# A product-key gate table built from three bf16 products per token instead of one fp32 product, and 64 instead of 48 expert chunks parked beside it

## The chip, the cores and the metric

One core of one Trainium2 chip. The time is the device time of one execution in microseconds (us), as the median of three runs. The engines are TensorE (PE in the rows; PEld is its weight load), VectorE (DVE), ScalarE (ACT), GpSimd (POOL) and SyncE (SP), which issues most DMAs.

## The reference

One transformer layer over 512 tokens of width 1024: attention and a gated recurrence in parallel, merged, then a product-key mixture of 16384 single-neuron experts (8 heads, 16 experts each per token), then a gated embedding. The part that matters here is the mixture:

```python
s = jnp.einsum('thpc,hpnc->thpn', q, sub_keys)      # 2 x 128 key scores per head
v1, i1 = lax.top_k(s[:, :, 0], 16)
v2, i2 = lax.top_k(s[:, :, 1], 16)
...                                                 # 16 best of the 256 sums: idx = 128 * i1 + i2
g = jax.nn.softmax(top_s, axis=-1)
ue = jnp.take(u, idx, axis=0)                       # 128 rows of u per token
a = jnp.einsum('thkd,td->thk', ue, x)
w = jax.nn.gelu(a) * g
ve = jnp.take(v, idx, axis=0)
out = jnp.einsum('thk,thkd->td', w, ve)
```

## The kernel before

The first 128 tokens take the mixture by gathering: for each of 128 slots an indirect DMA fetches one row of u per token (tile gu), VectorE multiplies and sums it (L849), and later the same with v (gv, L858). The other 384 tokens take it densely: all 16384 experts, in 128 chunks of 128, are computed for every token and multiplied by a gate table that is zero except at the chosen experts.

A dense chunk is `dense_a`: its weights (u_raw, 512 KB, 128x1024) are split by ScalarE into u_h and by VectorE into the rest u_l (`split`, L139 and L140), 24 fp32r matmuls of 384 columns (`mm3`, L134 to L136, three for each of 8 slices) fill the PSUM tile pa, and ScalarE's gelu (L742) writes ge, 128x384. The second half of a chunk, in the loop over `it` from 0 to 127, loads the rows of v, splits them, multiplies ge by the chunk's part of the gate table (gch, loaded for 8 chunks at a time from DRAM), splits the product into w_h and w_l, and adds 18 matmuls of 512 columns into six PSUM banks po.

The gate table must be whole before the second halves can start. While it is built, TensorE gets first halves of chunks to do: SP of them (48) are parked, that is, ge is written to DRAM (adram) and read back later (ges). The remaining 80 chunks have their first half inside the loop over `it`, up to 8 ahead (PRE). `chunk_order` spreads the parked chunks among the others.

The table is built in this order: `topk` (VectorE, tb 0 and 1: selection of the experts), then for each of the three blocks of 128 dense tokens `build`, with the selection of the next block woven in (`zipped`). In `build` a block is transposed (L811), and its first index, second index and gates land in tij and gr with the token on the free axis. For 8 tokens at a time (TQ), VectorE compares an iota with the first index (gL, fp32 one-hots, L823) and with the second (gO, bf16, L825), ScalarE multiplies each token's gO by its gate (gR, fp32, L827), and TensorE multiplies the two over the 128 slots: one fp32 matmul of 128 columns per token into pg (L832), which runs as two instructions in the trace. ScalarE copies pg, four tokens at a time, into gs (L834). After 32 tokens gs goes to DRAM (gdram, L836). pg, gL, gO and gR have two buffers each.

The loop over `units()` sets the order: each step of selection or building yields a cost, and a chunk is issued whenever the summed cost passes another APACE (3.3). Gathers of u are issued by the same sum. The generators' costs are not touched by the change. Within an engine, instructions run in their written order.

Of the kernel before, what the change touches and what calls it, by code (L numbers as in the profile page):

```python
# [8 lines left out]
F32 = mybir.dt.float32  # L9
F32R = mybir.dt.float32r  # L10
BF16 = mybir.dt.bfloat16
I32 = mybir.dt.int32
U32 = mybir.dt.uint32
AF = mybir.ActivationFunctionType
OP = mybir.AluOpType
# [16 lines left out]
GB = 32  # L32
# [14 lines left out]
TD = T - NG  # L47
NTB = TD // GB
PRE = 8
SP = 48  # L50
TQ = 8
APACE = 3.3
GPACE = 0.4
GSTART = 30
GS2 = 135
# [22 lines left out]
def chunk_order():  # L78
    spilled, fresh = [], []
    for c in range(128):  # L80
        ns, nf = SP - len(spilled), 128 - SP - len(fresh)
        (spilled if ns and (c < S0 or not nf or ns * (128 - SP) >= nf * SP) else fresh).append(c)
    return {c: i for i, c in enumerate(spilled)}, spilled + fresh
# [29 lines left out]
def zipped(*gens):  # L113
    gens = [[0.0, i, g] for i, g in enumerate(gens)]
    while gens:
        e = min(gens)
        try:
            c = next(e[2])
        except StopIteration:
            gens.remove(e)  # L120
            continue
        e[0] += c
        yield c


def body(nc, tc, I, out, taps=None, stop=99):
# [17 lines left out]
    with contextlib.ExitStack() as top:  # L144
# [563 lines left out]
        if stop <= 5:  # L708
            ul_st.close()
            return  # L710
        peer(nc, tc, I, out, xd, cst, gains, norm_T1, rstd_of, split, mm3, tap, stop, pp, ha, la, h2n, v8s, i8s, st, top,
             idxg, gg, acc, aa, ul_st, up, u_split, u_pre)


def peer(nc, tc, I, out, xd, cst, gains, norm_T1, rstd_of, split, mm3, tap, stop, pp, ha, la, h2n, v8s, i8s, st, top,
         idxg, gg, acc, aa, ul_st, up, u_split, u_pre):
    import contextlib
    V, S, PE, G, DM = nc.vector, nc.scalar, nc.tensor, nc.gpsimd, nc.sync
    ident = cst[:, C_ID:C_ID + 128]
    iota = cst[:, C_IOTA:C_IOTA + 128]  # L720
# [3 lines left out]
    if True:  # L724
        dp = st.enter_context(tc.tile_pool(name="gdram", bufs=1, space=bass.MemoryType.DRAM))
        gd = dp.tile([NTB, 128, 128 * GB], F32, name="gdram")
        ad = dp.tile([SP, 128, TD], F32, name="adram")
        ys = contextlib.ExitStack()
# [5 lines left out]
        def dense_a(c):  # L734
            uh, ul = u_pre.pop(c, None) or u_split(c)
            pa = psa.tile([128, TD], F32, name="pa", tag="pa")
            for k in range(ND):
                e = slice(k * 128, (k + 1) * 128)
                mm3(pa, uh[:, e], ul[:, e], ha[:, k, NG:T], la[:, k, NG:T], k == 0, k == ND - 1)
            ge = gp.tile([128, TD], F32, name="ge", tag="ge")  # L740
            with tc.high_priority(HPG):
                S.activation(ge, pa, AF.Gelu_apprx_tanh)  # L742
            return ge
# [64 lines left out]
        def build(kp, bp, ps, tb, i_f, g_o, iob):  # L808
            pt = ps.tile([128, 3, 128], F32, name="pt3", tag="pt3", bufs=1)
            for i, s in enumerate((i_f[:, 0, :], i_f[:, 1, :], g_o)):  # L810
                PE.transpose(pt[:, i, :], s, ident)  # L811
            tij = kp.tile([128, 2, 128], BF16, name="tij", tag="tij")
            S.activation(tij, pt[:, 0:2, :], AF.Copy)
            gr = kp.tile([128, 128], F32, name="gr", tag="gr")
            S.activation(gr, pt[:, 2, :], AF.Copy)
            for b in range(128 // GB):
                gs = bp.tile([128, 128, GB], F32, name="gs", tag="gs", bufs=1)
                for q8 in range(GB // TQ):
                    t0 = b * GB + q8 * TQ
                    LL = bp.tile([128, TQ, 128], F32, name="gL", tag="gL")  # L820
                    OO = bp.tile([128, 128, TQ], BF16, name="gO", tag="gO")
                    RR = bp.tile([128, TQ, 128], F32, name="gR", tag="gR")
                    V.tensor_tensor(LL, iob[:, :, 0][:, None, :].to_broadcast([128, TQ, 128]),  # L823
                                    tij[:, 0, t0:t0 + TQ, None].to_broadcast([128, TQ, 128]), op=OP.is_equal)
                    V.tensor_tensor(OO, iob, tij[:, 1, None, t0:t0 + TQ].to_broadcast([128, 128, TQ]), op=OP.is_equal)  # L825
                    for t in range(TQ):
                        S.activation(RR[:, t, :], OO[:, :, t], AF.Copy, scale=gr[:, t0 + t:t0 + t + 1])  # L827
                    for q4 in range(TQ // 4):
                        pg = ps.tile([128, 4, 128], F32, name="pg", tag="pg")
                        for w in range(4):  # L830
                            t = q4 * 4 + w
                            PE.matmul(pg[:, w, :], RR[:, t, :], LL[:, t, :], start=True, stop=True)  # L832
                        o = q8 * TQ + 4 * q4
                        S.activation(gs[:, :, o:o + 4].rearrange("p i t -> p t i"), pg, AF.Copy)  # L834
                    yield TQ * 0.21 + 0.1
                DM.dma_start(gd[(tb - TB0) * (128 // GB) + b], gs.rearrange("p i t -> p (i t)"))  # L836
# [25 lines left out]
        def gathers(nu, nv, dve=None, act=None):  # L862
            with tc.issue_after(dve.ins) if dve else contextlib.nullcontext():
                while cnt["u"] < min(128, nu):
                    slot_u(cnt["u"])
                    cnt["u"] += 1
            if nv is None:
                return
            while cnt["w"] < 128 and (cnt["u"] >= cnt["w"] + WG + WLAG or (cnt["u"] == 128 and nu >= 128 + WLAG)):
                with tc.issue_after(act.ins) if act else contextlib.nullcontext():  # L870
                    slot_w(cnt["w"])
                cnt["w"] += WG
            with tc.issue_after(dve.ins) if dve else contextlib.nullcontext():
                while cnt["v"] < min(cnt["w"], nv):
                    slot_v(cnt["v"])
                    cnt["v"] += 1

        with s7:
            kp = s7.enter_context(tc.tile_pool(name="topk", side="right", **LR))
            bp = s7.enter_context(tc.tile_pool(name="gbld", side="right", bufs=2, reuse_waits="tile"))  # L880
            ps = s7.enter_context(tc.psum_pool(name="psg", side="right", bufs=2, reuse_waits="tile"))
            iob = kp.tile([128, 128, TQ], BF16, name="iob")
            V.tensor_copy(iob, iota[:, :, None].to_broadcast([128, 128, TQ]))
            i16 = kp.tile([128, 16, NK], BF16, name="i16")
            V.tensor_copy(i16, iota[:, 0:16, None].to_broadcast([128, 16, NK]))

            def sel(tb):
                i_f = kp.tile([128, 2, NK], F32, name="i_f", tag="i_f", bufs=2)
                g_o = kp.tile([128, NK], F32, name="g_o", tag="g_o", bufs=2) if tb >= TB0 else gg
                sels[tb] = i_f, g_o  # L890
                yield from topk(kp, tb, i_f, g_o, i16)
                if tb < TB0:
                    idx_f = kp.tile([128, NK], F32, name="idx_f", tag="idx_f")
                    V.scalar_tensor_tensor(idx_f, i_f[:, 0, :], 128.0, i_f[:, 1, :], op0=OP.mult, op1=OP.add)
                    V.tensor_copy(idxg, idx_f)
                    tap("idx", idx_f)
                    tap("g", gg)

            sels = {}

            def units():
                yield from sel(0)
                yield from sel(1)
                for tb in (1, 2, 3):
                    gens = [build(kp, bp, ps, tb, *sels[tb], iob)]
                    if tb < 3:
                        gens.append(sel(tb + 1))
                    yield from zipped(*gens)

            na, cost = 0, 0.0  # L910
            pend = []

            def next_a(c):
                ge = dense_a(c)
                if c < SP:
                    DM.dma_start(ad[c], ge)
                else:
                    pend.append(ge)

            for _ in range(A0):  # L920
                next_a(na)
                na += 1
            for u in units():
                cost += u
                while cost > (na + 1 - A0) * APACE and na < SP + NPE:
                    next_a(na)
                    na += 1
                if cost > GSTART:
                    gathers((cost - GSTART) * GPACE + max(0.0, cost - GS2) * GP2, None)
            GW = cnt["u"]  # L930
            print("COST", cost, na, GW) if DBG else None
            while na < SP + NPE:
                next_a(na)
                na += 1
# [123 lines left out]
        with contextlib.ExitStack() as e2:  # L1058
            pe2.append(e2.enter_context(tc.tile_pool(name="ple3", side="right", **LR)))
            ps = e2.enter_context(tc.psum_pool(name="psp", side="right", bufs=4, reuse_waits="tile"))  # L1060
            for n in range(4):
                w = wg0 if n == 0 else load_wg(n)
# [60 lines left out]
```

## Time and profile before

| | us |
|---|---|
| median of three runs | 1925.13 |
| lowest and highest | 1924.31, 1926.99 |
| span of the profiled execution | 1926.0 |

The page gives the profiled execution by its span, from the first to the last instruction. By the stretches, the first 605 us are the projections, attention, recurrence and the queries; the selections and the table take until about 1010 us; the loop over `it` runs until about 1840 us; the embedding gate ends it. A busy time counts an instruction as long as it is recorded; matmuls overlap one another, so the distance between their starts says more than their length. Of a group, the mean length follows the busy time, and then the idle time of the engine just before, with what ended it.

### The profile page before, as it was taken

Reading aid. Unit: us, or ns where it says so; the run is one execution under the profiler, and the core shown is the slowest. Engines: PE = TensorE matmul, PEld = TensorE weight load, DVE = VectorE, ACT = ScalarE, POOL = GpSimd, SP = SyncE. Lnnn points to the kernel's source line nnn. Section 1 sums busy time; section 2 is a strip of 40 time slices with the busy share of each in tenths; the row PEclk is TensorE's granted clock in tenths of the full one; section 3 lists DMA queues with packets and bytes.
Section 4 is the critical chain, followed back from the end, with each engine's and each line's share of the span. In section 5 each row is a group of like instructions: output and inputs, shape, how many; then the busy total and the mean of one; then the engine's idle time right before and its main releaser. Section 6 shows DMA issues by size and latency. Waiting matters only on the chain.

```text
span 1926.0 us, 27936 instructions
## 1 busy us (share of the span) xinstructions
PE 1849.9 (96%) x10349; PEld 1641.7 (85%) x10349; DVE 1415.6 (73%) x2893; ACT 985.6 (51%) x1563; POOL 376.2 (20%) x260
## 2 busy tenths in 40 slices
PE   6999999999999999888889999999999999999998
PEld 6997878888998988777778889888888888888888
DVE  4689777444888999988746778877788777756464
ACT  5755657532533588998994333333333333333443
POOL 0000000000000222214200334444354443200000
PEclk9999999999999999999999999999999999999999
DMA  4212100433321776777749998988899888865512
GB/s 160 78 56 76 44 12 23 129 105 130 128 78 53 256 249 245 275 256 259 258 155 311 358 321 315 336 326 312 326 334 344 309 310 319 277 216 182 190 58 85
DMA packets 133944, 397.49 MB, mean 206 GB/s; under 512 B 12848, under 2 KB 52016, under 8 KB 132144
## 3 DMA queue, kind: packets, MB, share of 16 engines
q1 hardware_dynamic: 96944, 261.48, 39.4%
q0 software_dynamic: 36864, 134.23, 19.7%
q8 instruction: 81, 1.33, 0.3%
q14 instruction: 55, 0.45, 0.1%
HBM read 356.86 MB, written 38.80 MB: 205 GB/s over the span
## 4 chain that ended last, share of the span: by engine, by line
PE 46%; ACT 8%; DMA 2%; DVE 1%; issue 1%; ACTq 0%; SPq 0%
PE po L136 9%; PE po L135 9%; PE po L134 9%; PE pa L136 5%; PE pa L134 5%; PE pa L135 5%; ACT gR L827 4%; ACT gs L834 3%; DMA gdram<-gs 1%; ACT u_h L139 1%; PE pg L134 1%; PE pg L136 1%; PE pg L135 1%; DMA gchg<-gdram 1%; PE pg L832 0%
## 5 line engine op out<-in xcount | busy, mean ns | idle before, releaser
L843 POOL DMA_INDIRECT gu<-in_peer_u_dram,idxg x128 | 188.8, 1475 | 1137.5 <-DVE cd L766 662.9
L136 PE MATMUL pa<-ha,u_l 128*128 128x384 f32 x1024 | 349.6, 341 | 6.6 <-DVE u_l L140 6.6
L134 PE MATMUL pa<-ha,u_h 128*128 128x384 f32 x1024 | 349.4, 341 | 1.8 <-ACT u_h L139 1.8
L135 PE MATMUL pa<-la,u_h 128*128 128x384 f32 x1024 | 349.1, 341 | 0.0
L134 PE MATMUL po<-v_h,w_h 128*128 128x512 f32 x768 | 299.3, 390 | 1.8 <-ACT w_h L139 1.8
L135 PE MATMUL po<-v_l,w_h 128*128 128x512 f32 x768 | 300.8, 392 | 0.0
L136 PE MATMUL po<-v_h,w_l 128*128 128x512 f32 x768 | 300.7, 392 | 0.0
L139 ACT ACTIVATE u_h<-u_raw 128x1024 fp32r<-128x1024 f32 x128 | 136.1, 1064 | 203.4 <-PE pa L135 195.7
L843 POOL DMA_INDIRECT gv<-in_peer_v_dram,idxg x128 | 187.1, 1462 | 238.4 <-DVE acc L858 206.6
L140 DVE TENSOR_TENSOR u_l<-u_raw,u_h 128x1024 fp32r<-128x1024 f32 x128 | 156.3, 1221 | 89.5 <-ACT u_h L139 89.2
L136 PEld LDWEIGHTS pa<-ha,u_l 128*128 128x128 f32 x1024 | 193.7, 189 | 8.8 <-DVE u_l L140 8.5
L134 PEld LDWEIGHTS pa<-ha,u_h 128*128 128x128 f32 x1024 | 193.6, 189 | 5.2 <-ACT u_h L139 2.5
L135 PEld LDWEIGHTS pa<-la,u_h 128*128 128x128 f32 x1024 | 193.5, 189 | 2.7
L832 PE MATMUL pg<-gL,gR 128*128 128x128 f32 x768 | 146.7, 306 | 35.9 <-ACT gs L834 18.3
L140 DVE TENSOR_TENSOR v_l<-v_raw,v_h 128x1024 fp32r<-128x1024 f32 x128 | 155.9, 1218 | 23.3 <-ACT v_h L139 23.3
L827 ACT ACTIVATE gR<-gO,gr 128x128 f32<-128x128 bf16 x384 | 169.3, 539 | 4.6 <-DVE gO L825 4.6
L832 PEld LDWEIGHTS pg<-gL,gR 128*128 128x128 f32 x768 | 109.5, 192 | 72.8 <-ACT gR L827 34.2
L136 PEld LDWEIGHTS po<-v_h,w_l 128*128 128x128 f32 x768 | 144.7, 188 | 30.3
L134 PEld LDWEIGHTS po<-v_h,w_h 128*128 128x128 f32 x768 | 144.5, 188 | 30.5 <-ACT w_h L139 2.1
L135 PEld LDWEIGHTS po<-v_l,w_h 128*128 128x128 f32 x768 | 144.4, 188 | 28.7
L858 DVE SCALAR_TENSOR_TENSOR acc<-gv,aa,acc 128x1024 f32<-128x1024 f32 x128 | 163.7, 1279 | 6.1 <-DMA gv<-in_peer_v_dram,idxg 5.7
L849 DVE SCALAR_TENSOR_TENSOR gu<-gu,h2n 128x1024 f32<-128x1024 f32 x128 | 155.4, 1216 | 8.2 <-DMA gu<-in_peer_u_dram,idxg 8.2
(323 smaller groups left out, 3589.4 us busy)
## 6 DMA issues: line engine op xcount, KB each, us to landing
u_raw<-in_u_t_dram SPq DMA_DIRECT2D x128, 512.0 KB, 5.6
v_raw<-in_peer_v_dram SPq DMA_DIRECT2D x128, 512.0 KB, 6.8
gdram<-gs SPq DMA_DIRECT2D x12, 2048.0 KB, 8.1
gchg<-gdram SPq DMA_DIRECT2D x16, 1536.0 KB, 12.6
w_raw<-in_w_in_dram SPq DMA_DIRECT2D x42, 512.0 KB, 3.6
adram<-ge SPq DMA_DIRECT2D x48, 192.0 KB, 3.4
ges<-adram SPq DMA_DIRECT2D x48, 192.0 KB, 6.0
wq_raw<-in_peer_wq_dram SPq DMA_DIRECT2D x16, 512.0 KB, 3.6
```

The lines of the kernel that those rows point to most:

```text
L134: PE.matmul(ps, lh, rh, start=first, stop=False)
L135: PE.matmul(ps, lh, rl, start=False, stop=False)
L136: PE.matmul(ps, ll, rh, start=False, stop=last)
L139: ins = S.activation(hi, raw, AF.Copy)
L140: V.tensor_tensor(lo, raw, hi.bitcast(F32), op=OP.subtract)
L827: S.activation(RR[:, t, :], OO[:, :, t], AF.Copy, scale=gr[:, t0 + t:t0 + t + 1])
L832: PE.matmul(pg[:, w, :], RR[:, t, :], LL[:, t, :], start=True, stop=True)
L834: S.activation(gs[:, :, o:o + 4].rearrange("p i t -> p t i"), pg, AF.Copy)
L843: G.indirect_dma_start(out=t, out_offset=None, in_=src, in_offset=bass.IndirectOffsetOnAxis(ap=idxg[:, k:k + 1], axis=0))
L849: V.scalar_tensor_tensor(t, t, 1.0, h2n, op0=OP.mult, op1=OP.mult, accum_out=aa[:, k:k + 1])
L858: V.scalar_tensor_tensor(acc, t, aa[:, k:k + 1], acc, op0=OP.mult, op1=OP.add)
```

## The change

The gate of a token is written as the sum of three bf16 numbers: VectorE rounds it to bf16, subtracts, and does the same with the rest (g3). Both one-hots of 8 tokens are made by one comparison in bf16 (EE, 2048 elements per partition: 2 groups of 4 tokens, 2 indices, 128 keys, 4 tokens innermost). One multiplication by VectorE forms LG, the first index's one-hot times each of the three pieces (3072 elements). Per token TensorE adds three bf16 products into pg, with the second index's one-hot as weights each time; both operands have a step of four elements. ScalarE's scaling is gone. tij and gr get another order of elements. SP goes from 48 to 64 and APACE from 3.3 to 2.5.

```diff
--- before.py
+++ after.py
@@ -47,9 +47,9 @@
 TD = T - NG
 NTB = TD // GB
 PRE = 8
-SP = 48
+SP = 64
 TQ = 8
-APACE = 3.3
+APACE = 2.5
 GPACE = 0.4
 GSTART = 30
 GS2 = 135
@@ -809,28 +809,33 @@
             pt = ps.tile([128, 3, 128], F32, name="pt3", tag="pt3", bufs=1)
             for i, s in enumerate((i_f[:, 0, :], i_f[:, 1, :], g_o)):
                 PE.transpose(pt[:, i, :], s, ident)
-            tij = kp.tile([128, 2, 128], BF16, name="tij", tag="tij")
-            S.activation(tij, pt[:, 0:2, :], AF.Copy)
-            gr = kp.tile([128, 128], F32, name="gr", tag="gr")
-            S.activation(gr, pt[:, 2, :], AF.Copy)
+            tij = kp.tile([128, 32, 2, 4], BF16, name="tij", tag="tij")
+            S.activation(tij.rearrange("p q z t -> p z q t"), pt[:, 0:2, :].rearrange("p z (q t) -> p z q t", t=4), AF.Copy)
+            g3 = kp.tile([128, 32, 3, 4], BF16, name="g3", tag="g3")
+            gr = kp.tile([128, 32, 4], F32, name="gr", tag="gr")
+            S.activation(gr, pt[:, 2, :].rearrange("p (q t) -> p q t", t=4), AF.Copy)
+            for j in range(3):
+                V.tensor_copy(g3[:, :, j, :], gr)
+                if j < 2:
+                    V.tensor_tensor(gr, gr, g3[:, :, j, :], op=OP.subtract)
+            nq = TQ // 4
             for b in range(128 // GB):
                 gs = bp.tile([128, 128, GB], F32, name="gs", tag="gs", bufs=1)
                 for q8 in range(GB // TQ):
-                    t0 = b * GB + q8 * TQ
-                    LL = bp.tile([128, TQ, 128], F32, name="gL", tag="gL")
-                    OO = bp.tile([128, 128, TQ], BF16, name="gO", tag="gO")
-                    RR = bp.tile([128, TQ, 128], F32, name="gR", tag="gR")
-                    V.tensor_tensor(LL, iob[:, :, 0][:, None, :].to_broadcast([128, TQ, 128]),
-                                    tij[:, 0, t0:t0 + TQ, None].to_broadcast([128, TQ, 128]), op=OP.is_equal)
-                    V.tensor_tensor(OO, iob, tij[:, 1, None, t0:t0 + TQ].to_broadcast([128, 128, TQ]), op=OP.is_equal)
-                    for t in range(TQ):
-                        S.activation(RR[:, t, :], OO[:, :, t], AF.Copy, scale=gr[:, t0 + t:t0 + t + 1])
-                    for q4 in range(TQ // 4):
+                    q0 = (b * GB + q8 * TQ) // 4
+                    EE = bp.tile([128, nq, 2, 128, 4], BF16, name="gE", tag="gE")
+                    LG = bp.tile([128, nq, 3, 128, 4], BF16, name="gG", tag="gG")
+                    V.tensor_tensor(EE.rearrange("p q z i t -> p (q z) i t"), iob[:, None, :, :].to_broadcast([128, nq * 2, 128, 4]),
+                                    tij[:, q0:q0 + nq].rearrange("p q z t -> p (q z) t")[:, :, None, :].to_broadcast([128, nq * 2, 128, 4]),
+                                    op=OP.is_equal)
+                    V.tensor_tensor(LG, EE[:, :, 0:1].to_broadcast([128, nq, 3, 128, 4]),
+                                    g3[:, q0:q0 + nq, :, None, :].to_broadcast([128, nq, 3, 128, 4]), op=OP.mult)
+                    for q in range(nq):
                         pg = ps.tile([128, 4, 128], F32, name="pg", tag="pg")
-                        for w in range(4):
-                            t = q4 * 4 + w
-                            PE.matmul(pg[:, w, :], RR[:, t, :], LL[:, t, :], start=True, stop=True)
-                        o = q8 * TQ + 4 * q4
+                        for t in range(4):
+                            for j in range(3):
+                                PE.matmul(pg[:, t, :], EE[:, q, 1, :, t], LG[:, q, j, :, t], start=(j == 0), stop=(j == 2))
+                        o = q8 * TQ + 4 * q
                         S.activation(gs[:, :, o:o + 4].rearrange("p i t -> p t i"), pg, AF.Copy)
                     yield TQ * 0.21 + 0.1
                 DM.dma_start(gd[(tb - TB0) * (128 // GB) + b], gs.rearrange("p i t -> p (i t)"))
@@ -879,8 +884,8 @@
             kp = s7.enter_context(tc.tile_pool(name="topk", side="right", **LR))
             bp = s7.enter_context(tc.tile_pool(name="gbld", side="right", bufs=2, reuse_waits="tile"))
             ps = s7.enter_context(tc.psum_pool(name="psg", side="right", bufs=2, reuse_waits="tile"))
-            iob = kp.tile([128, 128, TQ], BF16, name="iob")
-            V.tensor_copy(iob, iota[:, :, None].to_broadcast([128, 128, TQ]))
+            iob = kp.tile([128, 128, 4], BF16, name="iob")
+            V.tensor_copy(iob, iota[:, :, None].to_broadcast([128, 128, 4]))
             i16 = kp.tile([128, 16, NK], BF16, name="i16")
             V.tensor_copy(i16, iota[:, 0:16, None].to_broadcast([128, 16, NK]))
```

## Rows read from the trace of the kernel before

**Rows 1.** The page, parts 1 and 2: busy shares, and tenths in 40 slices.

```profile
PE 1849.9 (96%) x10349; PEld 1641.7 (85%) x10349; DVE 1415.6 (73%) x2893; ACT 985.6 (51%) x1563; POOL 376.2 (20%) x260
PE   6999999999999999888889999999999999999998
ACT  5755657532533588998994333333333333333443
```

**Rows 2.** Table of stretches: us, busy us (x instructions) by engine, clock, DMA share, GB/s.

```profile
605.00:1010.00 405.00, 360.59 (x2074) 320.58 (x2073) 343.94 (x806) 345.82 (x614) 96.34 (x66) 0.98 0.67 235
690.00:960.00 270.00, 241.07 (x1383) 209.56 (x1382) 239.58 (x435) 253.80 (x470) 79.10 (x52) 0.99 0.74 258
960.00:1010.00 50.00, 43.00 (x261) 37.64 (x261) 24.54 (x19) 49.65 (x96) 0.00 (x0) 1.00 0.39 146
1030.00:1650.00 620.00, 618.20 (x3022) 549.99 (x3021) 486.34 (x614) 225.56 (x321) 261.16 (x177) 1.00 0.90 324
```

**Rows 3.** Groups, ScalarE, 690 to 1010 us: busy us, mean ns, idle before.

```profile
L827 ACT ACTIVATE gR<-gO,gr 128x128 f32<-128x128 bf16 x384 | 169.3, 539 | 4.6 <-DVE gO L825 4.6
L834 ACT ACTIVATE gs<-pg 128x512 f32<-128x512 f32 x96 | 103.2, 1118 | 5.8 <-DMA gdram<-gs 4.6 <-PE pg L832 1.2
L139 ACT ACTIVATE u_h<-u_raw 128x1024 fp32r<-128x1024 f32 x37 | 39.8, 1075 | 7.8 <-PE pa L135 6.9 <-ACT gs L834 0.8
L742 ACT ACTIVATE ge<-pa 128x384 f32<-128x384 f32 x36 | 17.9, 496 | 0.0
```

**Rows 4.** Waits, 690 to 1010 us: waiter and releaser, us, times, longest.

```profile
PEld pg L832 <- ACT gR L827: 34.2, 60, 2.3
PE pg L832 <- ACT gs L834: 18.3, 19, 2.0
PE pg L832 <- ACT gR L827: 15.8, 41, 1.9
```

**Rows 5.** Timeline of TensorE: start us, us, line, tiles, count.

```profile
250.00 0.61 PE L405 MATMUL pA<-DD,KK 128*128 128x128 f32 x4
...
600.10 0.28 PE L134 MATMUL pq<-ha,wq_h 128*128 128x256 f32 x1
600.22 0.28 PE L135 MATMUL pq<-la,wq_h 128*128 128x256 f32 x1
...
749.83 0.34 PE L135 MATMUL pa<-la,u_h 128*128 128x384 f32 x1
...
759.54 0.34 PE L134 MATMUL pa<-ha,u_h 128*128 128x384 f32 x1
...
761.68 1.24 PE L832 MATMUL pg<-gL,gR 128*128 128x128 f32 x6
```

**Rows 6.** Timeline of ScalarE from 764.55 us.

```profile
764.55 2.55 ACT L827 ACTIVATE gR<-gO,gr 128x128 f32<-128x128 bf16 x6
```

**Rows 7.** Stretches, first pa alone, then po alone.

```profile
605.00:1010.00 405.00, 262.01 (x1249) 217.97 (x1250) 25.01 (x51) 0.98 0.67 235
...
1030.00:1650.00 620.00, 391.97 (x1672) 314.23 (x1673) 0.00 (x0) 0.00 (x0) 1.00 0.90 324
```

**Rows 8.** Groups, VectorE, 690 to 1010 us.

```profile
L823 DVE TENSOR_TENSOR gL<-iob,tij 128x1024 f32<-128x1024 bf16 x48 | 96.4, 2008 | 18.8 <-PE pg L832 17.6 <-ACT tij L813 1.1
L140 DVE TENSOR_TENSOR u_l<-u_raw,u_h 128x1024 fp32r<-128x1024 f32 x36 | 44.1, 1225 | 16.0 <-ACT u_h L139 15.7
L825 DVE TENSOR_TENSOR gO<-iob,tij 128x1024 bf16<-128x1024 bf16 x48 | 32.8, 683 | 13.0 <-ACT gR L827 12.8
L796 DVE TENSOR_TENSOR eq<-i,rb 128x2048 bf16<-128x2048 bf16 x4 | 4.7, 1219 | 0.0
```

**Rows 9.** DMA issues (KB, us to landing), and the stretch 1060 to 1100 us.

```profile
adram<-ge SPq DMA_DIRECT2D x48, 192.0 KB, 3.4
ges<-adram SPq DMA_DIRECT2D x48, 192.0 KB, 6.0
...
1060.00:1100.00 40.00, 40.00 (x183) 33.77 (x182) 31.36 (x42) 14.02 (x18) 18.28 (x13) 1.00 0.99 365
```

## The prediction

> **What bounds the kernel now.** The page comes first: TensorE is busy for 96% of the span, and its row of slices is at 8 or 9 nearly everywhere, but in the 15th to 21st slices, where the gate table is built, ScalarE's row rises to 8 and 9 while it is at 3 in the long stage behind [rows 1]. So the limit isn't the same engine throughout, and the stages have to be read apart. The table of stretches does that [rows 2]. From 1030 to 1650 us TensorE is busy for 618.20 of 620 us with every other engine well below: there a matmul removed is time removed, as long as the DMA engines (share 0.90) can follow. From 605 to 1010 us, the stage that the change rewrites (below: the build stage, with the selection of the first tokens ahead of it), TensorE shows 360.59 of 405 us; in its last 50 us ScalarE is busy for 49.65 and VectorE for only 24.54.
>
> The groups of ScalarE from 690 to 1010 us say with what [rows 3]: 169.3 us go to the scaling of the one-hots (gR), 103.2 us to the eviction of the finished tables (gs), 57.7 us to the chunks' own split and gelu. The waits agree [rows 4]: what TensorE waits for there is gR and gs, 34.2, 18.3 and 15.8 us.
>
> TensorE's busy time hides more of the same. Six half-products pg starting at 761.68 us are shown as 1.24 us of work; less the 0.28 us that the record of a short matmul lasts, that is about 0.19 us from start to start [rows 5]. Yet the four half-products pA, of the same 128x128 fp32 shape, take (0.61 - 0.28) / 3 = 0.11 us each. The six gR in the ScalarE row come one per (2.55 - 0.54) / 5 = 0.40 us [rows 3, 6], which is the pace of a pair of pg. So pg is paced by gR, and a token's own price on TensorE is 2 x 0.11 = 0.22 us, 384 x 0.22 = 85 us in all, where the row of groups would say 146.7.
>
> A chunk (24 matmuls pa of 384 columns) has its price in the timeline: 57 consecutive ones start between 749.83 and 759.54 us, 9.71 / 56 = 0.1734 us apart [rows 5], or 4.16 us a chunk. In 605 to 1010 us there are 1249 of them, that is 52 chunks (the 48 parked and 4 that run early) or 216.6 us [rows 7]. Real work of TensorE in this stage is therefore 217 + 85 + about 6 (the last query matmuls, and transposes) = 308 of 405 us. Nearly 100 us are spent waiting for ScalarE. That is the reserve the change can reach.
>
> **The change part by part.** The profiled execution's span is 1926.0 us, 0.9 above the median of the three runs; the sum is made against 1926.0 and no correction is applied.
>
> *ScalarE, removed.* All 384 gR go, 169.3 us [rows 3]. The two evictions into bf16 and fp32 ahead of each block change only their order of elements, and gs stays as it is. Sixteen more chunks in the stage bring 16 x (1.075 + 0.496) = 25 us. ScalarE in 605 to 1010 us: 345.8 - 169.3 + 25 = 202 us [rows 2, 3]. It stops being the limit by a wide margin.
>
> *VectorE, exchanged.* Per 8 tokens gL (2008 ns) and gO (683 ns) go [rows 8]. In their place come EE, 2048 bf16 elements, and LG, 3072. The rows with bf16 on both sides and an inner step of one are gO (1024 elements, 683 ns) and eq (2048 elements, 1219 ns): (1219 - 683) / 1024 = 0.523 ns an element and 147 ns fixed. EE is then 1.22 us and LG 1.75 us, 2.97 us where 2.69 stood; 48 times that is 143 instead of 129 us. Splitting the weights takes three copies and two subtractions of 128 elements per block, three blocks, at 0.28 to 0.3 us about 4 us. The 16 chunks bring 16 x 1.225 = 20 us of u_l. VectorE in 605 to 1010 us: 343.9 - 129 + 143 + 4 + 20 = 382 us [rows 2, 8]. Against 405 us it had slack; now it is one of two candidates for the limit. That EE's and LG's second operand runs over 4 elements where gO's ran over 8 I cost at nothing; the other end is the third rival.
>
> *TensorE, exchanged.* A token had two half-products; it gets three bf16 products of 128 columns, each with its own 128x128 load, 1152 in all. The trace holds no bf16 matmul. From below: the 256-column matmuls pq start 0.12 us apart, the 384-column ones 0.1734 [rows 5], so 128 fewer columns are worth 0.053 us and 128 columns cost 0.12 - 0.053 = 0.067 us, if loading a half-size weight keeps up. From above: pA, with a 128x128 fp32 load per 128 columns, 0.11 us. Neither end allows a gain against 0.22 us a token except the lowest (3 x 0.067 = 0.20); the operands' step of four elements is in no row. The operation lies between the two in what it loads, half of pA's bytes, so I take the middle, 0.0885 us: 1152 x 0.0885 = 102 us, with 77 and 127 as ends. The exchange by itself thus costs TensorE some 17 us of work, and buys that this work no longer waits for gR.
> [...]
>
> *Sixteen chunks moved.* 16 x 4.16 = 67 us of TensorE leave the stage behind 1010 us and enter the build stage, with 16 loads u_raw. TensorE in 605 to 1010 us then holds 217 + 67 + 6 + 102 = 392 us of work (367 to 417).
>
> *Length of the build stage.* The limits are TensorE 392 and VectorE 382 us, side by side. How close a limiting engine comes to filling the stage is in the rows of before: ScalarE, the limit from 690 us on, filled 253.80 + 49.65 = 303.45 of 320 us, so the stage was 1.055 times its work [rows 2]. 392 x 1.055 = 413 us against 405: the stage gets 8 us longer and does 67 us more of matmuls.
>
> *Behind it.* TensorE was full there [rows 2], so 67 us come off in full if the transfers follow. What is added is 16 writes of ge (192 KB, 3.4 us to landing) inside the build stage and 16 reads of ges (6.0 us) behind it, all on SP's queue [rows 9]; in return 16 loads of 512 KB move forward. The writes fall where the DMA share is 0.67 [rows 2], so I cost them at nothing; the reads are prefetched four deep and their price is the second rival.
>
> Sum: 1926 + 8 - 67 = 1867 us.
>
> **The rivals.** *The load bounds the bf16 product* (0.11 us, as pA). TensorE's work in the stage is 417 us and the stage 417 x 1.055 = 440: 1926 + 35 - 67 = 1894 us. For it: pA's loads settle at 0.11, and each product has a load of its own, three in a row of the same one-hot. Against it: a 16-bit weight is half as large. [...]
>
> *The transfers stop following.* In 1030 to 1650 us the DMA engines move 324 GB/s at a share of 0.90 [rows 2], 201 MB. The 80 late chunks become 64. The stretch holds 1672 matmuls po, 93 iterations of 18, and 1350 others, 56 chunks of pa [rows 7]; a fifth of them, 11, go: 11 x 4.16 = 46 us less time, 11 x 0.524 = 5.8 MB less of u and 11 x 0.197 = 2.2 MB more of ges. That leaves 197.4 MB for 574 us, 344 GB/s, where a full share is 324 / 0.90 = 360. One stretch shows 365 GB/s at 0.99 with TensorE still full [rows 9], so there is room, but 4%. If the stage can't be fed faster than before, 197.4 MB at 324 GB/s take 609 us, 35 more: 1867 + 35 = 1902 us. TensorE would then have gaps in the long stage, ended by v_raw, gchg or a gather.
>
> *VectorE drops to one element a cycle or less* (the case on the other side). gL reads bf16 with an uneven step and takes 1.96 ns an element; the split u_l, fp32, takes 1.2 ns [rows 8]. If runs of four elements, or the threefold reading of EE, put EE and LG on u_l's rate, they cost 5120 x 1.2 = 6.1 us a unit instead of 2.97, VectorE has 382 + 48 x 3.1 = 531 us in the stage, and the stage is 531 x 1.055 = 560: 1926 + 155 - 67 = 2014 us. It decides from the point where the stage grows by the 67 us that were moved: 472 / 1.055 = 447 us of VectorE, or 2.97 + 65 / 48 = 4.3 us for the pair. Against it: gO reads with the same kind of broadcast and runs of 8 at the fast rate.
>
> *The relief isn't turned into matmuls.* Instructions run in their written order; a product that waits for LG holds the chunk behind it. If each of the moved chunks merely lengthens the stage by its own 4.16 us and the waits on ScalarE become waits on VectorE, it is 405 + 67 us long and the time stays at 1926. For it: VectorE's 382 us are unevenly spread, with two selections in the first two thirds (239.58 of 270 us there, 24.54 of 50 at the end [rows 2]). Against it: while VectorE is at work on one unit, TensorE has two thirds of a chunk per unit to do, and the chunks don't depend on EE or LG.
>
> **How the numbers follow.** The forecast, 1867 us, has 0.50; the load bound (1894) 0.20; the transfers (1902) 0.18; VectorE slow (2014) 0.07; no relief (1926) 0.05. The lower bound takes TensorE at 367 us, where VectorE's 382 is the limit and fills the stage wholly: 1926 - 23 - 67 = 1836, rounded to 1840. The upper bound takes in the load bound and the transfers, 1908. Out of it stay the last two rivals, 0.12, and the tails. Faster by over 0.2% (about what a measurement of this kernel can tell from no change): the first three, and a little of the last, 0.89. Within 0.2%: 0.04. Slower: 0.07.
>
> **What would show it.** Right: in the stage from about 605 to 1020 us no ACTIVATE on gR, ScalarE near 200 us, TensorE and VectorE both over 380 us, some 64 to 69 chunks before the table's last write instead of 52; behind it TensorE still full, with fewer pa among the same number of po. The price of a bf16 product can be read from consecutive pg: 0.067, 0.09 or 0.11 us apart. EE should show 1.22 and LG 1.75 us. Wrong: EE or LG above 2 and 3 us; pg waiting mostly for LG with VectorE idle before ScalarE's gs (two buffers of pg too few); gaps of TensorE after 1030 us ended by a DMA; a share of the DMA engines at 0.99 through the whole long stage.

## The result, and the profile after

| | before | after |
|---|---|---|
| median, us | 1925.2 | 1936.32 |
| lowest and highest | 1924.31, 1926.99 | 1933.67, 1937.13 |
| span of the profiled execution | 1926.0 | 1935.4 |

The ratio is 1.0053, 95% interval 1.004 to 1.0065: the change makes the kernel half a per cent slower, where 1867 us, 3% faster, was forecast.

The two stages, first by the table of stretches of the changed kernel (columns as in [rows 2]):

```profile
605.00:1048.00 443.00, 430.26 (x2828) 416.95 (x2827) 378.60 (x837) 231.68 (x260) 89.66 (x66) 0.99 0.69 240
1100.00:1500.00 400.00, 398.80 (x1926) 350.63 (x1925) 319.59 (x406) 140.23 (x198) 202.71 (x129) 1.00 0.94 344
1500.00:1750.00 250.00, 226.42 (x1053) 200.59 (x1052) 167.14 (x208) 77.20 (x108) 78.41 (x54) 0.95 0.79 275
```

The last two stretches of the kernel before:

```profile
1100.00:1500.00 400.00, 400.00 (x1981) 358.66 (x1980) 314.34 (x393) 143.01 (x201) 174.21 (x121) 1.00 0.91 326
1500.00:1750.00 250.00, 250.00 (x1239) 224.14 (x1238) 174.51 (x214) 88.12 (x125) 80.90 (x53) 1.00 0.80 275
```

The groups that make the table in the changed kernel, the eviction's row with its first and last start (from the view of the tile gs; the same row of the kernel before behind it), and the first 24 products on TensorE's timeline:

```profile
L831 DVE TENSOR_TENSOR gG<-gE,g 128x3072 bf16<-128x3072 bf16 x48 | 83.3, 1750 | 0.0
L828 DVE TENSOR_TENSOR gE<-iob,tij 128x2048 bf16<-128x2048 bf16 x48 | 58.6, 1220 | 24.6 <-PE pg L837 24.6
L837 PE MATMUL pg<-gG,gE 128*128 128x128 bf16 x1152 | 143.9, 297 | 4.8 <-DVE gG L831 2.5 <-ACT gs L839 2.3
L837 PEld LDWEIGHTS <-gE 128*128 128x128 bf16 x1152 | 129.1, 117 | 14.5 <-issue 9.6 <-DVE gG L831 2.3 <-DVE sm L803 0.2
...
L839 ACT ACTIVATE gs<-pg x96: 1063/1134/1200, 704.4 to 1048.1; 128x512 f32<-128x512 f32 x96
L834 ACT ACTIVATE gs<-pg x96: 1031/1110/1258, 695.1 to 1009.0; 128x512 f32<-128x512 f32 x96
...
702.83 2.98 PE L837 MATMUL pg<-gG,gE 128*128 128x128 bf16 x24 [1.20 <-DVE gG L831]
```

The build stage (605 us to the start of the table's last eviction) went from 404 to 443 us; ScalarE is at 231.68 there instead of 345.82 [rows 2], and VectorE's two new operations last what they should. The products start (2.98 - 0.30) / 23 = 0.117 us apart. Behind the stage 887 us are left, 30 less than before, where 67 less were due. Between 1500 and 1750 us TensorE is idle for 23.6 us, and the granted clock averages 0.95. The first of its five gaps there, of 4.64 us, shows both: behind it the clock is at 0.50 (1528 to 1530 us), and matmuls pa start 0.32 us apart; a little later it is back at 1.00 (1532 to 1534 us), and they start 0.17 us apart.

```profile
1527.41 0.69 PE L136 MATMUL pa<-ha,u_l 128*128 128x384 f32 x1 [4.64 <-DVE u_l L140]
...
1528.22 0.52 PE L135 MATMUL pa<-la,u_h 128*128 128x384 f32 x1
1528.54 0.52 PE L136 MATMUL pa<-ha,u_l 128*128 128x384 f32 x1
...
1532.33 0.33 PE L134 MATMUL pa<-ha,u_h 128*128 128x384 f32 x1
1532.50 0.33 PE L135 MATMUL pa<-la,u_h 128*128 128x384 f32 x1
...
1528.00:1530.00 2.00, 2.00 (x8) 2.00 (x7) 2.00 (x4) 0.00 (x0) 0.93 (x2) 0.50 0.77 197
1532.00:1534.00 2.00, 2.00 (x12) 1.91 (x11) 0.97 (x1) 0.61 (x1) 1.35 (x2) 1.00 1.02 280
```

At 0.95 of full speed over 250 us, by an estimate up to 250 x 0.05 = 12.5 us more are lost. Together up to 36 us: nearly all of the 37 us that are missing behind the stage, at one place.

What stands behind the gaps, by the waits of the changed kernel from 1500 to 1750 us (all engines, then VectorE's and TensorE's own), and the last of the five gaps on the timelines of VectorE, SP and TensorE:

```profile
ACT v_h L139 <- DMA v_raw<-in_peer_v_dram: 90.1, 22, 12.1
DVE ges L966 <- DMA ges<-adram: 59.7, 14, 9.6
PE pa L136 <- DVE u_l L140: 23.6, 5, 7.3
...
1694.12 0.55 DVE L140 TENSOR_TENSOR w_l<-ges,w_h 128x384 fp32r<-128x384 f32 x1
1694.59 1.22 DVE L140 TENSOR_TENSOR v_l<-v_raw,v_h 128x1024 fp32r<-128x1024 f32 x1
1695.72 1.28 DVE L863 SCALAR_TENSOR_TENSOR acc<-gv,aa,acc 128x1024 f32<-128x1024 f32 x1
1700.47 0.56 DVE L966 TENSOR_TENSOR ges<-ges,gchg 128x384 f32<-128x384 f32 x1 [3.47 <-DMA ges<-adram]
1700.94 1.28 DVE L863 SCALAR_TENSOR_TENSOR acc<-gv,aa,acc 128x1024 f32<-128x1024 f32 x1
1702.14 1.22 DVE L140 TENSOR_TENSOR u_l<-u_raw,u_h 128x1024 fp32r<-128x1024 f32 x1
...
1694.70 0.33 SPq L963 DMA_DIRECT2D ges<-adram  x1
...
1703.41 0.69 PE L136 MATMUL pa<-ha,u_l 128*128 128x384 f32 x1 [5.36 <-DVE u_l L140]
```

A reload of ges is issued at 1694.70 us, just after w_l has freed one of the four buffers; 2.3 us of other work later VectorE stands before the product ges x gchg and waits 3.47 us for that reload. TensorE waits for u_l, which stands behind the product in VectorE's order. This is the rule in that stretch: with each reload paired with its product on the timelines, VectorE reaches the median one of 22 products from 1450 to 1750 us 2.3 us after the issue of its reload. In the kernel before (18 products) it is 17.4 us.

The reloads of ges are VectorE's largest wait there, but not its only one. Two of the five gaps, 11.9 of the 23.6 us, come right behind a wait of 8.38 us before the same product for which the profile shows no releaser, and one of 9.22 us for gchg, the gate columns of the next eight chunks.

### The profile page after: what moved, and what is told of

It reads as the page before. It is cut to its first block, busy times and chain, and to the rows that moved or that the text cites. A ratio compares the mean times of both kernels' runs of the same rounds, so it can differ in the third digit from the quotient of the medians.

```text
span 1935.4 us, 28360 instructions
## 1 busy us (share of the span) xinstructions
PE 1864.6 (96%) x10733; PEld 1680.7 (87%) x10733; DVE 1427.0 (74%) x2908; ACT 847.5 (44%) x1179; POOL 379.8 (20%) x260
## 4 chain that ended last, share of the span: by engine, by line
PE 33%; issue 11%; DMA 9%; DVE 8%; POOL 2%; ACT 1%; DVEq 0%; POOLq 0%; ACTq 0%; SPq 0%
PE po L136 5%; PE po L135 5%; PE po L134 5%; PE pa L136 4%; PE pa L134 4%; PE pa L135 4%; PE pg L837 4%; DMA gchg<-gdram 3%; DMA ges<-adram 3%; DVE acc L863 2%; POOL gu L848 2%; DVE gu L854 1%; DVE v_l L140 1%; DVE u_l L140 1%; DMA gu<-in_peer_u_dram,idxg 1%
## 5 line engine op out<-in xcount | busy, mean ns | idle before, releaser
L848 POOL DMA_INDIRECT gu<-in_peer_u_dram,idxg x128 | 178.5, 1394 | 1168.6 <-DVE cd L766 652.0
L848 POOL DMA_INDIRECT gv<-in_peer_v_dram,idxg x128 | 201.2, 1572 | 218.6 <-DVE acc L863 187.5
L139 ACT ACTIVATE v_h<-v_raw 128x1024 fp32r<-128x1024 f32 x128 | 134.4, 1052 | 156.1 <-DMA v_raw<-in_peer_v_dram 143.4
L966 DVE TENSOR_TENSOR ges<-ges,gchg 128x384 f32<-128x384 f32 x64 | 35.3, 554 | 163.9 <-DMA gchg<-gdram 81.4
L837 PE MATMUL pg<-gG,gE 128*128 128x128 bf16 x1152 | 143.9, 297 | 4.8 <-DVE gG L831 2.5
```

The costliest lines, as they stand in the source:

```text
L139: ins = S.activation(hi, raw, AF.Copy)
L837: PE.matmul(pg[:, t, :], EE[:, q, 1, :, t], LG[:, q, j, :, t], start=(j == 0), stop=(j == 2))
L848: G.indirect_dma_start(out=t, out_offset=None, in_=src, in_offset=bass.IndirectOffsetOnAxis(ap=idxg[:, k:k + 1], axis=0))
L966: mi = V.tensor_tensor(ge.rearrange("p (b t) -> p b t", t=GB), ge.rearrange("p (b t) -> p b t", t=GB), gch[key][:, :, c % GC, :], op=OP.mult)
```

## The experiments

Labels give the order in which they ran. Two questions were separate from the start: what makes the product cost 0.117 us, and what makes the gaps in the loop.

### The two halves of the change, each alone

```diff
 # e1: the changed kernel
-SP = 64
-APACE = 2.5
+SP = 48
+APACE = 3.3
```

> The new table with 48 chunks parked and the old pace of 3.3: the table change alone. Theory: the build stage is bound by TensorE, a bf16 product costs 0.118 us, and the loss behind 1100 us belongs to the parking. Then TensorE holds 217 + 136 + 6 = 359 us in the stage, it ends at about 605 + 359 / 0.97 = 975 us instead of 1010, and the loop behind it is as before: about 1891 us, 35 less than before. Rival (the loss in the loop comes with the earlier or denser table, not with the parking): the stage ends early too, but the loop behind it grows, 1915 to 1930 us.

```diff
 # e2: the kernel before
-SP = 48
-APACE = 3.3
+SP = 64
+APACE = 2.5
```

> The old table with 64 chunks parked and the pace of 2.5: the parking alone. Theory: the build stage stays bound by ScalarE, which gets 25 us more, so it ends at about 1035 to 1040 us; the loop behind shows the same gaps of TensorE from about 1500 us as the changed kernel and takes its 886 us: about 1921 us. Rival (the loop's gaps come with the new table's timing, not with the parking): the loop takes 849 us, about 1885 us.

The table alone: 1927.78 us, ratio 1.0015 (1.0005 to 1.0024). The parking alone: 1939.56 us, ratio 1.007 (1.0046 to 1.0095). Neither half gains; both together lose 0.5%. The stage of e1 with a wait of VectorE and one of TensorE in it, and then the loop of e2 with its largest wait of VectorE from 1500 to 1750 us:

```profile
605.00:1014.00 409.00, 377.79 (x2492) 362.78 (x2491) 358.58 (x823) 211.30 (x232) 96.75 (x66) 0.95 0.68 234
DVE gE L828 <- PE pg L837: 27.1, 13, 5.1
PE pa L134 <- ACT ge L742: 11.6, 8, 2.8
```

```profile
1500.00:1750.00 250.00, 226.50 (x1067) 199.43 (x1067) 167.83 (x209) 78.09 (x110) 80.09 (x55) 0.96 0.81 281
DVE ges L961 <- DMA ges<-adram: 57.8, 14, 11.0
```

In e1 the loop is as before, so the loss there belongs to the parking; e2 confirms it, with the same 23.5 us of gaps and the same wait. It came out 18 us above its forecast of 1921, since its table ends at 1051 us and not at 1035 to 1040. And e1's stage did not get shorter: 409 us where 370 were expected. TensorE's real work there (about 1276 pa at 0.1734 us, 1152 products at 0.117, 6) is 362 us and VectorE's 358.58, each 0.88 of the stage, where TensorE's work filled 0.95 of the changed kernel's. Neither is full: VectorE waits 27.1 us until products free a one-hot tile, and TensorE is idle for 31 us, 24.5 of them behind ScalarE (11.6 for ge), although ScalarE is busy for little more than half of the stage. That two limits of equal size leave each other no backlog is a reading of these waits; e9, below, tests it from one side. The granted clock is lower too, 0.95 on average where the changed kernel has 0.99; 16 of the 47 us that TensorE's work leaves are not idle time, and by an estimate the clock accounts for up to 409 x 0.05 = 20 us. How much of the loss would stay at a full clock was not tested. The expectation, which took one limit's work divided by 0.97, failed on that.

### Which operand makes the product slow

```diff
 # e3: weights
-PE.matmul(pg[:, t, :], EE[:, q, 1, :, t], LG[:, q, j, :, t], ...)    # ...: start and stop as they were
+PE.matmul(pg[:, t, :], EE[:, q, 1].rearrange("p i t -> p (i t)")[:, 128 * t:128 * t + 128], LG[:, q, j, :, t], ...)
 # e4: moving operand
-PE.matmul(pg[:, t, :], EE[:, q, 1, :, t], LG[:, q, j, :, t], ...)
+PE.matmul(pg[:, t, :], EE[:, q, 1, :, t], LG[:, q, j].rearrange("p i t -> p (i t)")[:, 128 * t:128 * t + 128], ...)
```

> The changed kernel with the weights of each product read as 128 elements in one run instead of one in four (the table then holds other values). Theory (the load sets the price whatever the step, as with the fp32 loads at 0.11): consecutive products stay at 0.118 us, table ends at about 1048 us. Rival (the step of four elements makes the load slow): about 0.065 us a product, 1152 x 0.053 = 61 us less work of TensorE in the stage, table ends at 1000 us or before, where VectorE's 382 us set the limit.

> The changed kernel with the moving operand of each product read as 128 elements in one run instead of one in four (the table then holds other values), weights as in the changed kernel. Theory (the load sets the price): 0.118 us a product, no change. Rival (the step of the moving operand sets it): about 0.065 us, the table ends at 1000 us or before.

One run each, in which the table gets other values: 1929.41 us (e3) and 1896.96 us (e4). 24 products of e3, then of e4, on TensorE's timeline:

```profile
704.33 2.94 PE L837 MATMUL pg<-gG,gE 128*128 128x128 bf16 x24 [1.18 <-DVE gG L831]
```

```profile
772.21 1.53 PE L837 MATMUL pg<-gG,gE 128*128 128x128 bf16 x24
```

With one run of weights the products are still (2.94 - 0.29) / 23 = 0.115 us apart. With one run of the moving operand it is (1.53 - 0.22) / 23 = 0.057 us. So the step of the moving operand alone halves the rate, and the load, strided as it was, keeps up with 0.057 us. The clock is not the reason: in the changed kernel it is at 1.00 from 702 to 708 us, and in e3 and e4 the last matmuls pa ahead of these products start 0.17 us apart, as they do at 1.00. The theory that the load sets the price is refuted, and with it the reason that the first rival gave for its nearly right number. The table of e4 ends at 1006 us, with VectorE busy for 0.93 of the stage. Why e3 is some 7 us below the changed kernel was not followed up; its table ends at 1047 us.

The records of single loads last 117 ns in the changed kernel and 115 ns in e4, but they overlap: e4 has one load per product, 1152 of each, and starts a product every 0.057 us. The length of a load's record is not its price per product.

### Two tokens innermost

```diff
-EE = bp.tile([128, TQ // 4, 2, 128, 4], BF16, ...)
-LG = bp.tile([128, TQ // 4, 3, 128, 4], BF16, ...)
+EE = bp.tile([128, TQ // 2, 2, 128, 2], BF16, ...)
+LG = bp.tile([128, TQ // 2, 3, 128, 2], BF16, ...)
 # tij, g3, gr and iob the same way; the products take tokens 2 * q + t // 2, t % 2
```

> The changed kernel with two instead of four tokens innermost in the one-hots: both operands of a product have a step of two elements, 4 bytes, VectorE's elements stay the same in number. Theory (the moving operand's step of 8 bytes halves the rate of columns; 4 bytes are what every fp32 operand here has, at full rate): consecutive products are 0.055 to 0.065 us apart, EE and LG stay at 1.22 and 1.75 us, the table ends at about 1006 us and the whole takes about 1897 us, like the run with the moving operand in one run. Rivals: any step but one halves the rate, 0.118 us and 1935 us; or runs of two elements put VectorE on one element a cycle, EE 2.3 and LG 3.4 us, the table ends after 1110 us, 1990 us or more.

1889.66 us, ratio 0.9793 (0.9757 to 0.9828); its four runs lie between 1879.50 and 1897.30, wider apart than those of the others. TensorE's timeline and VectorE's groups:

```profile
711.34 1.55 PE L837 MATMUL pg<-gG,gE 128*128 128x128 bf16 x24
...
L831 DVE TENSOR_TENSOR gG<-gE,g 128x3072 bf16<-128x3072 bf16 x48 | 83.4, 1752 | 0.0
L828 DVE TENSOR_TENSOR gE<-iob,tij 128x2048 bf16<-128x2048 bf16 x48 | 58.3, 1221 | 4.3 <-PE pg L837 4.3
```

A step of two is as good as a step of one, 0.058 us against 0.057 in e4, and VectorE loses nothing with runs of two elements: 1.221 and 1.752 us, where half the rate of [rows 8] (2 x 0.523 ns an element and 147 ns) would have been 2.3 and 3.4. The one change of layout turns the loss of 0.5% into a gain of about 2%.

### The gaps in the loop

```diff
+gm = vp.tile([128, TD], F32, name="gm", tag="gm", bufs=1)
 # the rearranges of gm and ge are left out here
-mi = V.tensor_tensor(ge, ge, gch[key][:, :, c % GC, :], op=OP.mult)
+mi = V.tensor_tensor(gm, ge, gch[key][:, :, c % GC, :], op=OP.mult)
-ai = split(ge, wh, wl)
+ai = split(gm, wh, wl)
```

> The changed kernel, in which the product of a chunk's ge with its gate column is written to a tile of its own with one buffer, instead of back into ge. Theory A (order): with 64 chunks parked, VectorE makes these products up to eight chunks before they are wanted, as far as the four buffers of ges reach; each waits for a reload that was issued some 4 us before, and VectorE, which works in order, holds up the splits of v and u behind it that TensorE needs now. With one buffer for the product it can't run ahead, a ges buffer is free a chunk after its load was used, the reloads are issued 40 us early: the gaps of TensorE behind 1500 us vanish, the loop takes about 850 us instead of 886, the whole 1900 us. Theory B (bandwidth: the loop moves about as much as the DMA engines can): the gaps stay, 1930 to 1936 us.

```diff
+held = {}                      # ahead of slot_v(k)
-t = gather(vn, k, "gv")
+if k % 2 == 0:
+    held["v"] = gather(vn, k, "gv")
+t = held["v"]
```

> The changed kernel without every second gather of v (a slot then uses the row of the slot before it); VectorE's work is the same, the loop moves 34 MB less, some 15%. Theory A (order): reloads still wait on buffers that early products hold; the gaps behind 1500 us stay for the larger part, 1920 us or more. Theory B (bandwidth): the gaps vanish, about 1900 us.

The tile of its own (e5): 1912.70 us, ratio 0.9931 (0.9914 to 0.9948), 24 us below the changed kernel. Half the gathers of v (e6): 1905.38 us in one run, which leaves out every second gather of v. The stretch from 1500 to 1750 us and VectorE's longest wait in it, of e5 and then of e6:

```profile
1500.00:1750.00 250.00, 250.00 (x1221) 221.98 (x1220) 191.97 (x234) 88.98 (x125) 85.05 (x64) 1.00 0.88 307
DVE w_l L140 <- ACT w_h L139: 34.7, 22, 2.3
```

```profile
1500.00:1750.00 250.00, 245.70 (x1193) 218.35 (x1192) 177.22 (x218) 86.88 (x121) 48.53 (x31) 0.99 0.71 237
DVE ges L970 <- DMA ges<-adram: 50.5, 17, 8.2
```

e5 moves the same bytes, 307 instead of 275 GB/s in that stretch, with TensorE full and the wait for ges gone: its reloads are issued 57 to 72 us ahead of their products. So the DMA engines could move more than they did: bandwidth alone did not make the gaps. e6 leaves the order alone, VectorE still reaches the median product 2.3 us after the issue of its reload and waits 50.5 us for ges, and yet TensorE's gaps shrink to 4.3 us. So theory A in its strict form, by which e6 should have stayed at 1920 us, falls as well. What both runs leave standing is a product of the two: reloads issued some 2 us ahead of an in-order engine, times the time they take to land under load (in 1450 to 1750 us a median of 6.1 us in the changed kernel, 4.5 in e6). Taking away either takes most of the gaps away. That 9 us less of VectorE's wait for ges are worth 19 us of TensorE's gaps in e6 was not followed up, nor what the waits for gchg have to do with either run. e5 did not reach its 1900: it has a new gap of 6.2 us between 1100 and 1200 us, where TensorE waits for w_h, w_h for the product, and the product 3.9 us for gchg.

### Both repairs, and what each needs

e8 is e7 and e5 together; e9 is e7 with 48 chunks parked and the old pace; e10 is the kernel before with e5's tile; e11 is e2 with e5's tile; e12 is e8 with `SP = 80` and `APACE = 2.0`.

> Both: two tokens innermost, and the product of ge and gate in a tile of its own. Theory (two separate causes, 61 us of TensorE's work in the build stage and 35 us of gaps in the loop, whose effects add): 1935 - 38 - 35 = about 1862 us, faster than the kernel before by some 3%. Rival (they are the same loss: whatever the table gains is lost in the loop): about 1895 us.

> The table with two tokens innermost, 48 chunks parked, pace 3.3: the fast product without the parking. Theory: the table alone with step four brought nothing because TensorE and VectorE were both at some 360 us in a stage of 409 and neither filled it; with the fast product TensorE has 217 + 66 + 6 = 289 us, VectorE's 362 are the only limit, the stage is 362 / 0.95 = 381 us long, the table ends at 986 us and the loop is as before: about 1902 us. Rival (without more chunks the stage's length is set by the chain from one-hot to eviction, whatever the product costs): 1925 us, as the table alone.

> The kernel before with the product of ge and gate in a tile of its own. Theory (with 48 parked the loop's TensorE is full whatever VectorE waits for): same time, 1920 to 1930 us. Rival (early products cost the kernel before as well): 1910 us or less.

> The old table with 64 chunks parked and the product in a tile of its own. Theory: the gaps behind 1500 us go, as with the new table, some 24 us off the parking alone (1939.6): about 1915 us; the table still ends near 1051 us, since ScalarE sets it, so less than 1% is gained on the kernel before. Rival (the new table is needed for the loop to gain): 1935 us or more.

> Two tokens innermost, the product in a tile of its own, and 80 chunks parked at a pace of 2.0. In the build stage TensorE then has 350 + 67 = 417 us and VectorE 382 + 20 = 402. Theory: TensorE becomes the limit again, 417 / 0.945 = 441 us, so the stage grows by 41 us and the loop can save 67 at most: 1840 us if the loop follows. Rival (the loop can't follow: with 48 late chunks it asks for about 370 GB/s, more than any long stretch has shown): the loop's gaps come back, 1865 to 1900 us.

| run | what | us | ratio, 95% interval |
|---|---|---|---|
| e8 | step of two, own tile, 64 parked | 1868.30 | 0.9694 (0.9675 to 0.9712) |
| e9 | step of two, 48 parked | 1895.85 | 0.9851 (0.9834 to 0.9867) |
| e10 | the kernel before, own tile | 1925.36 | 1.0003 (0.9993 to 1.0012) |
| e11 | old table, own tile, 64 parked | 1922.05 | 0.9990 (0.9974 to 1.0005) |
| e12 | as e8, 80 parked | 1870.68 | 0.9719 (0.9702 to 0.9736) |

The build stage of e8, of e9 and of e12 (each until the table's end):

```profile
605.00:1005.00 400.00, 370.78 (x2832) 354.80 (x2830) 375.12 (x837) 222.18 (x261) 94.37 (x66) 0.99 0.75 266
```

```profile
605.00:980.00 375.00, 324.63 (x2485) 305.59 (x2484) 357.46 (x823) 201.97 (x232) 99.30 (x66) 0.94 0.73 254
```

```profile
605.00:1061.00 456.00, 428.14 (x3149) 411.12 (x3148) 393.18 (x850) 238.78 (x286) 96.32 (x66) 0.99 0.72 256
1100.00:1500.00 400.00, 390.13 (x1826) 337.64 (x1825) 319.47 (x413) 136.10 (x198) 184.90 (x125) 0.98 0.95 342
```

The repairs add up: 47 and 24 us apart, 68 together, and e8 is 3% faster than the kernel before. e9 shows that the table with the fast product gains 29 us with no more chunks parked than before; VectorE alone fills 0.95 of that stage, at a clock of 0.94. e10 shows that with 48 chunks parked the early products cost nothing. In e11, without the new table, the parking breaks even: ScalarE still sets the stage (the last eviction starts at 1053 us), and its loop has TensorE full from 1500 us on, but 5 us of gaps ahead of that, and 1915 us were expected. e12 gains nothing over e8, where 1840 us were expected: the stage takes 56 us more, not 41, and eats the 53 us that the shorter loop saves, 10 us of gaps being back in it from 1100 to 1500 us. There again two engines are close together, TensorE at about 408 us of work (1940 pa, 1152 products, 6) and VectorE at 393, 0.89 and 0.86 of 456 us.

## Why the prediction was wrong

*What bounds the kernel* held: ScalarE paced the build stage through gR, and without gR the wait went away (231.68 us of ScalarE in 443, and 2.3 us in which the products wait for its gs). The 202 us put down for ScalarE were 30 too low: the 169.3 us of gR are the sum of records that overlap (539 ns each, 0.40 us apart), and e1, without gR, has 345.82 - 211.30 = 134.5 us less of ScalarE. That cost nothing, as ScalarE was not the limit any more.

*VectorE, exchanged* held: EE 1.220 us (forecast 1.22), LG 1.750 (1.75), 378.60 us in the stage (382). The third rival is named after one element a cycle; no run shows a cycle of VectorE, and its price is u_l's 1.2 ns an element [rows 8], where EE and LG showed 0.60 and 0.57.

*TensorE, exchanged* is the first step that failed. The product was put between 0.067 and 0.11 us and taken at 0.0885; it cost 0.117, outside both ends. The prediction said that the operands' step of four was in no row, and then gave that unknown no price: both ends came from rows whose moving operand is contiguous. It weighed the load instead, which e3 and e4 show to be no limit at either rate. A contiguous moving operand costs 0.057 us (e4), below the lower end: the prices of both layouts lie outside the two ends, one on each side. 1152 x (0.117 - 0.0885) = 33 us. The rest of this term held: 1627 pa by 1050 us against 68 chunks (1632), and a stage of 443 us for 280 + 135 + 6 = 421 us of work, 0.95, where 0.948 was assumed.

*Behind it, the reads prefetched four deep* is the second. Four buffers are four deep only if they are free. The waits of the kernel before from 1050 to 1850 us have the row:

```profile
DVE ges L961 <- DMA ges<-adram: 19.2, 9, 4.7
```

TensorE's backlog hid these 19.2 us: its own waits there sum to 0.3 us. With 48 parked every 2.7th chunk takes a buffer, with 64 every second, and the loop has 67 us less of TensorE's work to hide the wait. The rival for this (the transfers stop following, 35 us) came out near its price, 37 us, by luck. Its mechanism, the whole loop held to 324 GB/s, did not occur: from 1100 to 1500 us the changed kernel moved 344 GB/s with TensorE full, and where TensorE starved the DMA share was 0.79. Of its signs the gaps came, ended by u_l behind VectorE's waits for ges, which it did not name, and for gchg, which it did.

*The rivals as alternatives* is the third. The load bound (plus 27 us) and the transfers (plus 35) were given chances of 0.20 and 0.18 as cases that exclude each other, and the range ended just above the worse one (1902), at 1908. What they stood for lies in different stages and so adds: 1867 + 33 + 37 = 1937, against 1935.4 measured in the profile. A range over independent terms has to reach their sum. The forecast "faster" at 0.89 rested on no two of them coming together.

*The relief isn't turned into matmuls*, given 0.05, is close to the measured time by luck. By it the stage grows by the whole 67 us and the loop keeps its gain; measured, the stage grew by 39 us, in part since the new table is more work for TensorE (135 us against the 85 that the half-products needed), and the loop lost 37 of its 67.

## What to carry to other kernels

Ask for each new operand which dimension the engine streams, and price its step from a row with that step, or leave the price open upwards; here a layout that was good for VectorE (four tokens innermost, LG 1750 ns) halved the rate of TensorE's columns (0.117 us a product), and half of it (two) served both (1752 ns, 0.058 us). When work is moved out of a saturated stage, list what that stage's slack was hiding: VectorE's early products cost nothing with 48 chunks parked, when TensorE had a backlog (e10, ratio 1.0003 without them), and 24 us with 64 (e5). Add up the bad cases that lie in different stages, and take 0.88 rather than 0.95 as the filling of a stage in which two engines carry nearly the same work (0.88 in e1, 0.89 in e12).

## What the runs showed of the hardware

A bf16 matmul of 128 columns, with a load of its own, started every 0.117 us when its moving operand stepped by four elements (8 bytes; the changed kernel), every 0.058 with two (e7) and every 0.057 with one (e4). The granted clock was at 1.00 around those of the changed kernel (702 to 708 us), and ahead of those of e4 and e7 fp32r matmuls of 384 columns started 0.17 us apart, as they do at 1.00. The weights' step of four cost nothing that shows: 0.057 us with it in e4, and only 0.002 us between the changed kernel and e3. VectorE's bf16 operations kept their rate with a broadcast operand in runs of four and of two elements (1750 and 1752 ns for 3072 elements, the changed kernel and e7). In the changed kernel TensorE's granted clock was at 0.50 after a gap of 4.64 us (1528 to 1530 us), and fp32r matmuls of 384 columns started 0.32 us apart; at 1.00 (1532 to 1534 us) they started 0.17 us apart.
